# Two more weight slots, in room that GpSimd's transfer scratch held: one layer of gated mixers and experts on one core

## The chip, the core and the metric

The kernel runs on one core of a Trainium2 chip. The metric is the device time of one execution in microseconds (us), taken as the median of several runs. A profile is one further execution, recorded instruction by instruction. The engines are PE (matrix products), DVE (vector), ACT (scalar), POOL (GpSimd) and SP (which here only issues transfers).

## The reference, cut to what matters

Sequence 256, width 1024, one layer: two token mixers side by side, then 32 experts in 4 groups, of which each token takes the best group and in it the best two experts.

```
h = rmsnorm(x, norm1_g)
u, v_a, q, k, v_b = split(h @ w_in)              # w_in 1024 x 5120
y_a = chunked_spatial_gating(u, v_a, ...)        # u * (tril(w_s) rmsnorm(v) + b), chunks of 128
y_b = rmsnorm(diff_attention(rms(q), rms(k), v_b)) * (1 - lam_init)
g_a, g_b = split(sigmoid(h @ w_gate + b_gate))
merged = g_a * (y_a @ w_up_a) + g_b * (y_b @ w_up_b)
x = x + merged @ w_out
h2 = rmsnorm(x, norm2_g)
x = x + hierarchical_moe(h2, w_rg, b_rg, w_re, b_re, w1, w3, w2)
# expert e: ((silu(h2 @ w1[e]) * (h2 @ w3[e])) * c[e]) @ w2[e], 1024 -> 256 -> 1024, all in float32
```

## The kernel before, in words

All weights are read once: 136 chunks of 1 MB (128 partitions x 2048 float32, 8 KB per partition), 40 of the dense products (`wf`) and 96 of the experts (`wm`: 8 groups of 4 experts, 12 chunks each, of which 8 hold w1 and w3 and 4 hold w2). I number the experts' chunks c0 to c95, so that group g has c(12g) to c(12g+11).

Room on chip is a list of slots of 8 KB per partition, handed out in the order in which they came free. `NSLOT = 20` slots are there from the start; 3 of them serve the split halves of weights (`hl`), the other 17 serve chunks, x and its parts, and `hl` as well when the three are taken. Later parts of the program add slots where other buffers end. `Stream.pump(reserve)` issues the next chunk's load on SP's queue as long as more than `reserve` slots are free; RESERVE gives that number phase by phase, 6 at the start and 0 or 1 later. So how far the loads run ahead of the products is the number of slots, and the order in which they stand in SP's queue is fixed when the program is written out (a manual schedule). SP's transfers use eight semaphores in turn, so that a load is issued only when the load eight places ahead of it has landed. Room that the gates leave is handed on as four pieces of 2 KB, and a chunk that goes there is loaded by four transfers of 256 KB (line 121); all other chunks go by line 123, and the very last one by two halves (line 115).

The program has two stages. In the dense stage (to about 269 us) every product is made in three passes: a half chunk (a unit) is split into `hl`, the high part by ACT (line 339), the low part by DVE (line 343), of units 12 to 43 the last 352 columns by POOL (line 345). PE uses both in lines 355 to 359 and 384 to 386. Attention heads, norms and constants are hung between the units. `wst`, the spatial mixer's weights, is loaded at unit AT by line 239, and POOL masks it in line 244 and makes further constants in lines 245 to 249, ahead of its next part of a split.

In the expert stage PE gathers a group's tokens (line 976), makes h from 8 chunks (line 1025, 8 products a chunk), turns `hid` (`pt`, line 1039), makes y from 4 chunks (line 1067, 16 products a chunk) and adds it to the result (line 1046). A chunk's slot is handed back right after its products, and the next load is issued there. In the last group 20 small products on constants follow each chunk of h (`wps`, line 215) and 10 more the last, which keep PE at work. `pv` holds the gains per partition, 128 x 43; ACT's first split of x (line 306) reads it.

```
    def pump(self, reserve):
        while self.i < len(self.srcs) and len(self.slots.free) > reserve:
```

Of the kernel before, what the change touches and what calls it, by code (L numbers as in the profile page):

```python
# [5 lines left out]
F32 = mybir.dt.float32  # L6
F32R = mybir.dt.float32r
BF16 = mybir.dt.bfloat16
# [7 lines left out]
P = 128  # L16
D = 1024
# [6 lines left out]
NWARM = 35          # products before the first operands are there  # L24
GLO, GPART = (12, 44), 352      # units of whose low parts GpSimd makes so many columns
# places of the steps of an attention head, in units of the dense products
# [9 lines left out]
NSLOT = 20          # slots of 8 KB per partition  # L36
RESERVE = (6, 3, 2, 0, 0, 0, 0, 0, 1)     # slots kept free of weights, phase by phase
SL = 32             # token slots of an expert in a round
NW = (20, 10)
# columns of the result in the weight chunks of w2: the last chunk comes and is used in two parts, on different banks  # L40
COLS = (((0, 256),), ((512, 256),), ((256, 128), (768, 128)), ((384, 128), (896, 128)))
NGRP = 8            # groups of four experts on the tensor engine
NCH = 12            # weight chunks of a group
ROUNDS = T // SL

# columns of the per-partition vectors
# [3 lines left out]
class Slots:  # L50
    """Slots of 8 KB per partition, handed out in the order in which they were freed; some are four pieces of 2 KB."""
# [21 lines left out]
    def take_chunk(self):  # L73
        """Room for a weight chunk, as tile or as four."""
        if isinstance(self.free[0][1], str):
            return self.take([P, 2048], F32, "w")
        s = self.free.pop(0)
        self.k += 1
        t = tuple(s[0].tile([P, 512], F32, tag=tag, name=f"w_{self.k}_{i}") for i, tag in enumerate(s[1]))
        self.owner[id(t)] = (s, t)  # L80
        return t
# [5 lines left out]
    def give(self, other):  # L87
        """All free slots to another."""
        other.free += self.free
        self.free = []  # L90


def piece(chunk, e):
    """An expert's part of a weight chunk."""
    return chunk[e] if isinstance(chunk, tuple) else chunk[:, e * 512:(e + 1) * 512]


class Stream:
    """Loads of weight chunks, issued in order as slots become free."""
# [6 lines left out]
    def pump(self, reserve):  # L106
        while self.i < len(self.srcs) and len(self.slots.free) > reserve:
            src = self.srcs[self.i]
            if self.i == len(self.srcs) - 1:        # in columns, to be used one after the other
                if all(not isinstance(tag, str) for _, tag in self.slots.free):  # L110
                    break
                t = self.slots.take([P, 2048], F32, "w")
                c = 0
                for _, w in COLS[-1]:
                    self.nc.sync.dma_start(t[:, c * 8:(c + w) * 8], src[:, c * 8:(c + w) * 8])
                    c += w
            else:
                t = self.slots.take_chunk()
                if isinstance(t, tuple):
                    for e in range(4):  # L120
                        self.nc.sync.dma_start(t[e], src[:, e * 512:(e + 1) * 512])
                else:
                    self.nc.sync.dma_start(t, src)
            self.ready.append(t)
            self.i += 1

    def claim(self):
        """A slot for the next chunk, whose load the caller issues."""
        t = self.slots.take([P, 2048], F32, "w")
        self.ready.append(t)  # L130
        self.i += 1
        return t
# [16 lines left out]
def body(tc, cp, sp, tp, mmp, axp, xT_d, xn_d, wf_d, wm_d, wst_d, bs_d, pv_d, rb_d, wr_d, out_d):  # L149
# [11 lines left out]
    # Pools of a part of the program, on memory that others use before and after.  # L161
# [22 lines left out]
    stream = Stream(nc, slots, [wf_d[i] for i in range(40)] + [wm_d[g, c] for g in range(NGRP) for c in range(NCH)])  # L184
    pv = cp.tile([P, PV_N], F32, name="pv")
    nc.gpsimd.dma_start(pv, pv_d)
# [18 lines left out]
    # the tensor engine's clock rises while it works: let it, before the first operands are there  # L205
# [16 lines left out]
    # key - query for the keys of the first query tile, then of the second; far below zero where masked  # L222
# [6 lines left out]
    utri = cp.tile([P, P], BF16, name="utri")   # 1 where row < column  # L229
# [12 lines left out]
    def late_consts():  # L242
        # causal mask of the spatial weights: s <= t
# [12 lines left out]
    em = cp.tile([P, NT], F32, name="em")       # EPS / r1^2, r1 the first norm's factor  # L256
    rbc = fp.tile([P, T], F32, name="rbc")      # r1 along the free axis, on all partitions
    nlam = cp.tile([P, 1], F32, name="nlam")    # -(lambda)
# [51 lines left out]
    # A unit takes half a weight chunk, split two units ahead. Other work is queued for a unit's place.  # L310
# [50 lines left out]
    def add_nat(ab, name, done, res, pre=None):  # L361
        """512 columns of a product, tokens on partitions: a result for each token tile."""
# [10 lines left out]
    def add_T(ab, name, done, res, pre=None):  # L373
        """256 columns of a product, columns on partitions: [P, 2, T]."""
# [16 lines left out]
    def norm_a(pss, name):  # L391
        """Squares of pss."""
        sqs = []
        for t in range(len(pss)):
            sq = t2k([P, 512], f"sq_{name}{t}")
            S.activation(sq, pss[t], AF.Square)
            sqs.append(sq)
        return sqs

    def norm_r(sqs, n, d, scaled, name):  # L400
        """1 / root mean square of the n groups of d in the rows, of their squares; scaled: of rows still to be multiplied by r1,
        with that factor (r1 rsqrt(r1^2 ss / d + EPS) = rsqrt(ss / d + EPS / r1^2))."""
# [51 lines left out]
    KL = 3 * P      # keys of the first query tile, then those of the second  # L454
    TS = (slice(0, P), slice(P, KL))

    def attn_head(h, off):
        st = {}

        def s0():  # L460
            sc = st["sc"] = qp.tile([P, 2, KL], F32, tag="t3k", name=f"sc{h}", bufs=2)
            pss = [ax_ps(f"sc{h}{c}") for c in range(2)]
            for t in range(NT):     # the two halves side by side, on 64 rows each
# [193 lines left out]
    def swap():  # L657
# [6 lines left out]
        def park(half):  # L664
            """x into PSUM, until the residual is added."""
# [9 lines left out]
        # gates, pair of columns by pair; the merged product takes their place  # L675
# [35 lines left out]
    def to_router():  # L711
        """The memory of the temporaries: a slot, and the router's weights."""
# [20 lines left out]
    def x1_T(t, half, pts):  # L733
        """The transpose of half a token tile of x1, by way of parts of PSUM."""
# [14 lines left out]
    def o_done(pss):  # L749
        def a():  # L750
            A["acc"] = slots.take([P, NT, D], F32, "acc")   # x, then x + out, then that / rms
# [23 lines left out]
    res = [[None] * 2 for _ in range(NT)]       # the result, summed up in PSUM  # L775

    def res_init(t, half):
        """x1 into the result; x1 / rms, without the gain, takes its place."""
# [12 lines left out]
    def choose(t):  # L791
        """Steps of the choice of group and experts."""
# [43 lines left out]
    for q in range(4):      # the second half: only split here  # L836
        units.append(Unit(q % 2, None, None, None, 1 if q == 1 else RESERVE[8]))

# [44 lines left out]
    def gates_free(j):  # L883
        """Half of the merged product's memory, for weights."""
# [3 lines left out]
    # the first token tile is finished earlier than the second  # L888
# [4 lines left out]
    tail[0]()       # x + out, first half  # L893
# [5 lines left out]
    tail[1]()       # and its transposes  # L899
# [23 lines left out]
    def choice_end(sel, gather0, evac0):  # L923
        """The end of the choice of experts, of the second token tile mostly, and the first group's first half."""
# [26 lines left out]
    def put_out(c, n):  # L951
        """n columns of the result."""
# [10 lines left out]
    def group(g, chunks, done, mid, store):  # L963
        """Gathers the tokens of group g, in parts; then its products."""
# [30 lines left out]
        def gather0(t, part):  # L995
            """The first half in two parts, token tile by tile: the bank is cleared by the first product only."""
# [23 lines left out]
        def products():  # L1020
# [32 lines left out]
            for i, ranges in enumerate(COLS):  # L1053
# [3 lines left out]
                for part in [(r,) for r in ranges] if final else [ranges]:  # L1057
# [19 lines left out]
                    if store and i < 2:     # no other work to wait for  # L1077
# [33 lines left out]
    def consume(st):  # L1111
        """The next chunk of a stream; and what gives its slot back and loads ahead."""
# [13 lines left out]
    def rest():  # L1126
        for t in range(NT):
            weights(t)
        # number of further rounds
# [29 lines left out]
def prep(i):  # L1159
# [7 lines left out]
    def nat(w, nb):   # 512 columns -> 2 chunks [128, 4 kc, 512]  # L1167
        return w[:, nb * 512:(nb + 1) * 512].reshape(2, 4, P, 512).transpose(0, 2, 1, 3).reshape(2, P, 2048)

    def tr(w):        # -> chunks [128, 2 cc, 8 kc, 128]  # L1170
# [8 lines left out]
    wm = np.empty((NGRP, NCH, P, 4, 2, 256), np.float32)        # w1 and w3, then w2  # L1179
# [3 lines left out]
    w2 = A("w2")[..., cols].reshape(NGRP, 4, 2, P, 4, 256).transpose(0, 4, 3, 1, 2, 5)   # g, chunk, p, e, f, 256  # L1183
# [3 lines left out]
    for _, n in COLS[-1]:     # the last chunk's parts one after the other  # L1187
# [32 lines left out]
```

## Time and profile before

| | us |
|---|---|
| median of 3 runs | 475.11 |
| the runs | 476.5, 475.11, 473.06 |
| profiled execution, span | 469.4 |
| PE busy in it | 439.8 (94%) |
| DVE, ACT, POOL busy | 208.4, 175.4, 92.0 |
| chain that ended last | PE 66%, DMA 29% |
| read from HBM | 147.14 MB, mean 316 GB/s |

The profiled execution has no time of its own beside its span: the span runs from the first instruction to the last, and 5.7 us lie between it and the median of the runs (475.11 - 469.4). A share of busy time is a mean over both stages, which have different limits; the rows further down are therefore taken stretch by stretch. In them "out<-in" names tiles, "x8" counts instructions of one kind in a row, and what stands in brackets is the engine's idle time ahead of the first of them and what ended it.

### The profile page before, as it was taken

To read this page: it belongs to the slowest core of one execution; us is meant where nothing else is said; L and a number is where in the kernel's file an instruction comes from. 1 tells how busy PE (TensorE), PEld (TensorE's weight loads), DVE (VectorE), ACT (ScalarE), POOL (GpSimd) and SP (SyncE) were. 2 spreads that over 40 slices of the span, in tenths; PEclk is the share of its full clock that TensorE was granted. 3 is DMA by queue.
4 is the path that set the end of the run, shared out by engine and by line. 5 is a ranking of instruction groups with operands and counts; after the bars stand their busy time and mean duration, and the time that the engine had idled before them with its cause. 6 is when DMAs were issued, how large, how long until landed. Compare 5 with 4: busy or idle time off the path is not lost.

```text
span 469.4 us, 8478 instructions
## 1 busy us (share of the span) xinstructions
PE 439.8 (94%) x3446; PEld 335.5 (71%) x3446; DVE 208.4 (44%) x389; ACT 175.4 (37%) x332; POOL 92.0 (20%) x119
## 2 busy tenths in 40 slices
PE   8999999999999999999999988989889898959984
PEld 7878778878999999999988734554636464426553
DVE  4575687779897555555775641011111111110012
ACT  6646657776554664433455322010101010001001
POOL 2047665455757000003000100000000000000000
PEclk9999999999999999999999999999999999998998
DMA  7999960540237967788676989999999999999993
GB/s 252 371 422 417 420 278 5 181 177 2 90 96 276 417 220 271 311 318 345 243 305 265 339 342 426 419 422 406 416 420 418 422 406 420 420 421 420 405 381 94
DMA packets 28206, 148.81 MB, mean 317 GB/s; under 512 B 3184, under 2 KB 6016, under 8 KB 12160
## 3 DMA queue, kind: packets, MB, share of 16 engines
q1 hardware_dynamic: 28128, 148.18, 79.6%
q8 instruction: 29, 0.48, 0.4%
q14 instruction: 17, 0.14, 0.1%
q0 software_dynamic: 32, 0.02, 0.1%
HBM read 147.14 MB, written 1.05 MB: 316 GB/s over the span
## 4 chain that ended last, share of the span: by engine, by line
PE 66%; DMA 29%; DVE 2%; ACT 1%; SPq 1%; issue 1%; ACTq 0%; DVEq 0%
DMA w<-in_wm_dram 24%; DMA w<-in_wf_dram 5%; PE h L1025 4%; PE y L1067 3%; PE res L1046 3%; PE gp L976 2%; PE wps L215 2%; PE v L355 2%; PE u L384 2%; PE a L385 2%; PE a L384 2%; PE gb L384 2%; PE ga L386 2%; PE b L386 2%; PE b L385 2%; PE b L384 2%
## 5 line engine op out<-in xcount | busy, mean ns | idle before, releaser
L343 DVE TENSOR_TENSOR hl<-w,hl 128x1024 fp32r<-128x1024 f32 (+2 forms) x88 | 91.2, 1040 | 62.7 <-ACT hl L339 62.2
L339 ACT CAST hl<-w 128x1024 fp32r<-128x1024 f32 (+1 forms) x88 | 84.6, 969 | 83.8 <-PE a L386 12.8
L1025 PE MATMUL h<-w,hT 128*32 128x512 f32 x512 | 62.4, 599 | 4.2 <-DMA w<-in_wm_dram 4.2
L984 DVE TENSOR_TENSOR hT<-gp,pv 128x512 f32<-128x512 f32 (+1 forms) x19 | 11.3, 606 | 103.0 <-PE gp L976 103.0
L345 POOL TENSOR_TENSOR hl<-w,hl 128x352 fp32r<-128x352 f32 x32 | 40.7, 1278 | 23.7 <-ACT hl L339 21.2
L1067 PE MATMUL y<-w,hidT 128*32 128x256 f32 (+1 forms) x528 | 34.6, 391 | 5.0 <-issue 3.7
L1073 ACT COPY yy<-y 128x256 f32<-128x256 f32 (+1 forms) x33 | 12.1, 366 | 70.1 <-PE y L1067 70.0
L976 PEld LDWEIGHTS gp<-Sg,acc 128*128 128x128 f32 x256 | 30.4, 192 | 9.2 <-issue 8.0
L1011 POOL TENSOR_TENSOR Sw<-Sg,C 128x128 f32<-128x128 f32 x16 | 6.1, 399 | 157.0 <-PE res L1046 142.7
L1046 PE MATMUL res<-yy,SwT 128*128 128x128 f32 (+1 forms) x192 | 34.8, 324 | 1.1 <-ACT yy L1073 1.0
L1046 PEld LDWEIGHTS res<-yy,SwT 128*128 128x128 f32 x192 | 25.9, 191 | 12.3 <-issue 6.7
L976 PE MATMUL gp<-Sg,acc 128*128 128x128 f32 x256 | 32.1, 279 | 2.1 <-DVE Sg L972 2.1
L1025 PEld LDWEIGHTS h<-w,hT 128*32 128x32 f32 x512 | 13.0, 109 | 29.2 <-issue 15.7
L1067 PEld LDWEIGHTS y<-w,hidT 128*32 128x32 f32 x528 | 16.0, 112 | 17.4 <-issue 8.7
L1035 ACT ACTIVATE hid<-h 128x256 f32<-128x256 f32 x8 | 3.1, 383 | 59.0 <-PE h L1025 59.0
L1036 DVE TENSOR_TENSOR hid<-hid,h 128x256 f32<-128x256 f32 x8 | 3.4, 422 | 35.7 <-ACT hid L1035 35.7
L384 PE MATMUL u<-xh,hl 128*128 128x256 f32 x64 | 18.8, 293 | 0.0
L215 PEld LDWEIGHTS <-ones_b 128*128 128x128 bf16 x205 | 13.2, 106 | 7.8 <-issue 6.7
L384 PE MATMUL ga<-xh,hl 128*128 128x256 f32 x64 | 18.2, 285 | 0.0
L386 PE MATMUL ga<-xh,hl 128*128 128x256 f32 x64 | 18.1, 283 | 0.0
L386 PE MATMUL b<-ybh,hl 128*128 128x256 f32 x64 | 18.1, 283 | 0.0
L386 PE MATMUL a<-yah,hl 128*128 128x256 f32 x64 | 18.1, 283 | 0.0
(220 smaller groups left out, 957.3 us busy)
## 6 DMA issues: line engine op xcount, KB each, us to landing
w<-in_wm_dram SPq DMA_DIRECT2D x87, 1024.0 KB, 12.6
w<-in_wf_dram SPq DMA_DIRECT2D x36, 1024.0 KB, 9.5
w<-in_wm_dram SPq DMA_DIRECT2D x32, 256.0 KB, 9.0
w<-in_wf_dram SPq DMA_DIRECT2D x8, 256.0 KB, 4.5
w<-in_wf_dram SPq DMA_DIRECT2D x4, 512.0 KB, 8.7
xT<-in_xT_dram SPq DMA_DIRECT2D x8, 128.0 KB, 4.5
xn<-in_xn_dram SPq DMA_DIRECT2D x1, 1024.0 KB, 9.2
xs<-in_xn_dram SPq DMA_DIRECT2D x1, 1024.0 KB, 8.9
```

The costliest lines, as they stand in the source:

```text
L215: TE.matmul(wps[:, :P], ones_b, ones_b, start=True, stop=True)
L339: S.copy(hl[:, 0, c], raw[:, c])
L343: V.tensor_tensor(hl[:, 1, c.start:m], raw[:, c.start:m], hl[:, 0, c.start:m].bitcast(F32), ALU.subtract)
L345: G.tensor_tensor(hl[:, 1, m:c.stop], raw[:, m:c.stop], hl[:, 0, m:c.stop].bitcast(F32), ALU.subtract)
L384: TE.matmul(o, wh, ah[:, kc], start=kc == 0, stop=False)
L385: TE.matmul(o, wh, al[:, kc], start=False, stop=False)
L386: TE.matmul(o, wl, ah[:, kc], start=False, stop=kc == KC - 1)
L976: TE.matmul(ps[:, i * P:(i + 1) * P], h2[:, t, kc * P:(kc + 1) * P], st["S"][:, t].rearrange("p e s -> p (e s)"), start=start, stop=t == N ...
L1025: TE.matmul(ps[e * SL:(e + 1) * SL], st["h"][kc // 4][:, kc % 4, e * SL:(e + 1) * SL], piece(w, e), start=kc == 0, stop=kc == KC - 1)
L1046: TE.matmul(res[t][c // 512][:, c % 512:c % 512 + n], st["SwT"][:, t * P:(t + 1) * P], yy[:, o:o + n], start=False, stop=True, skip_group_ ...
L1067: TE.matmul(py[e * SL:(e + 1) * SL, :n], hidT[:, f, e * SL:(e + 1) * SL], w[e][:, f], start=f == 0, stop=f == 1)
L1073: S.copy(yy, py[:, :n])
```

## The change

Three edits. The memory that the program sets aside for descriptors of transfers issued by GpSimd goes from 16 KB per partition (the default) to 1 KB. The load of `pv`, the only transfer that GpSimd issued, is issued on ACT's queue instead. And NSLOT goes from 20 to 22, so that two more slots of 8 KB lie in what was scratch. The rest of the diff takes comments out and changes no line number.

```diff
-NSLOT = 20          # slots of 8 KB per partition
+NSLOT = 22
...
     pv = cp.tile([P, PV_N], F32, name="pv")
-    nc.gpsimd.dma_start(pv, pv_d)
+    nc.scalar.dma_start(pv, pv_d)
     xT = slots.take([P, KC, T], F32, "xT")
...
-    nc = _bacc.Bacc("TRN2", target_bir_lowering=False, num_devices=1)
+    nc = _bacc.Bacc("TRN2", target_bir_lowering=False, num_devices=1, dynamic_dma_scratch_size=1024)
```

On ACT, at the start of the program, the load of `pv` now comes first; the table load and the copy `warm_a` are there only to have the activation table in place:

```order
 L1216 UNCONDITIONAL_BRANCH
+L186 DMA pv<-in_pv_dram 128x43
 L210 ACT_TABLE_LOAD
 L210 COPY warm_a<-warm_a 128x1
```

It moved from POOL, whose first instruction after the constants of the frame it was. No other instruction changed its engine.

On SP, before, ten chunks by line 123 (they follow the four chunks that the start loads by halves and quarters) stand ahead of `wst`:

```order
L123 DMA w_260<-in_wf_dram 128x2048
L123 DMA w_281<-in_wf_dram 128x2048
L123 DMA w_304<-in_wf_dram 128x2048
L123 DMA w_306<-in_wf_dram 128x2048
L123 DMA w_308<-in_wf_dram 128x2048
L123 DMA w_341<-in_wf_dram 128x2048
L123 DMA w_378<-in_wf_dram 128x2048
L123 DMA w_454<-in_wf_dram 128x2048
L239 DMA wsb_109<-in_wst_dram 128x1024
```

Now, from the same load (the third by line 123) on:

```order
L123 DMA w_260<-in_wf_dram 128x2048
L123 DMA w_262<-in_wf_dram 128x2048
L123 DMA w_264<-in_wf_dram 128x2048
L123 DMA w_285<-in_wf_dram 128x2048
L123 DMA w_308<-in_wf_dram 128x2048
L123 DMA w_310<-in_wf_dram 128x2048
L123 DMA w_312<-in_wf_dram 128x2048
L123 DMA w_345<-in_wf_dram 128x2048
L123 DMA w_382<-in_wf_dram 128x2048
L123 DMA w_458<-in_wf_dram 128x2048
L239 DMA wsb_109<-in_wst_dram 128x1024
```

Two chunks more stand ahead of `wst`, twelve in place of ten; the numbers in names only count tiles.

On SP, before, the loads ahead of the router's bias and weights (`rb`, `wr`, near the end of the dense stage) are the last three dense chunks and six of the experts':

```order
L123 DMA w_1933<-in_wf_dram 128x2048
L123 DMA w_1964<-in_wf_dram 128x2048
L123 DMA w_2025<-in_wf_dram 128x2048
L123 DMA w_2086<-in_wm_dram 128x2048
L123 DMA w_2118<-in_wm_dram 128x2048
L123 DMA w_2120<-in_wm_dram 128x2048
L123 DMA w_2151<-in_wm_dram 128x2048
L123 DMA w_2211<-in_wm_dram 128x2048
L123 DMA w_2217<-in_wm_dram 128x2048
L719 DMA rb<-in_rb_dram 128x40
L720 DMA wr<-in_wr_dram 128x320
```

Now, at the same place:

```order
L123 DMA w_1937<-in_wf_dram 128x2048
L123 DMA w_1968<-in_wm_dram 128x2048
L123 DMA w_2029<-in_wm_dram 128x2048
L123 DMA w_2090<-in_wm_dram 128x2048
L123 DMA w_2122<-in_wm_dram 128x2048
L123 DMA w_2124<-in_wm_dram 128x2048
L123 DMA w_2155<-in_wm_dram 128x2048
L123 DMA w_2215<-in_wm_dram 128x2048
L123 DMA w_2221<-in_wm_dram 128x2048
L719 DMA rb<-in_rb_dram 128x40
L720 DMA wr<-in_wr_dram 128x320
```

The same number of loads stands there, but each is of a chunk two places further on in the sequence. This holds for the rest of the program: before, 23 of the experts' chunks are loaded ahead of the first load that follows an expert product (line 1025), now 25.

## Rows read from the trace of the kernel before

**Rows 1.** The page's part 2: 40 slices of equal length, first to last.

```profile
PEclk9999999999999999999999999999999999998998
...
GB/s 252 371 422 417 420 278 5 181 177 2 90 96 276 417 220 271 311 318 345 243 305 265 339 342 426 419 422 406 416 420 418 422 406 420 420 421 420 405 381 94
```

**Rows 2.** Busy time of engines, granted clock, DMA share, GB/s, by stretch.

```profile
270.00:281.00 11.00, 8.94 (x70) 3.58 (x63) 4.67 (x25) 3.15 (x8) 0.80 (x2) 1.00 0.88 339
...
308.00:419.00 111.00, 99.31 (x936) 55.34 (x940) 13.42 (x30) 10.84 (x29) 3.78 (x10) 1.00 1.02 417
419.00:434.00 15.00, 13.23 (x118) 7.83 (x122) 1.54 (x3) 1.87 (x5) 0.75 (x2) 0.89 1.01 421
```

**Rows 3.** PE's timeline, 372 to 435 us: start, duration, instruction, idle before.

```profile
372.91 0.44 PE L1039 MATMUL pt<-ident,hid 128*128 128x128 f32 x2 [1.02 <-DVE hid L1036]
...
394.45 0.44 PE L1039 MATMUL pt<-ident,hid 128*128 128x128 f32 x2 [1.02 <-DVE hid L1036]
395.52 1.93 PE L1067 MATMUL y<-w,hidT 128*32 128x256 f32 x32 [0.63 <-issue]
...
408.97 1.07 PE L1025 MATMUL h<-w,hT 128*32 128x512 f32 x8 [0.40 <-DMA w<-in_wm_dram]
411.45 1.06 PE L1025 MATMUL h<-w,hT 128*32 128x512 f32 x8 [1.42 <-DMA w<-in_wm_dram]
413.94 1.07 PE L1025 MATMUL h<-w,hT 128*32 128x512 f32 x8 [1.43 <-DMA w<-in_wm_dram]
...
418.91 1.07 PE L1025 MATMUL h<-w,hT 128*32 128x512 f32 x8 [0.93 <-DMA w<-in_wm_dram]
421.00 0.44 PE L1039 MATMUL pt<-ident,hid 128*128 128x128 f32 x2 [1.02 <-DVE hid L1036]
422.07 3.80 PE L1067 MATMUL y<-w,hidT 128*32 128x256 f32 x32 [0.63 <-DVE hidT L1041]
...
433.68 1.07 PE L1025 MATMUL h<-w,hT 128*32 128x512 f32 x8
```

**Rows 4.** The chain that ended last, in order of time: start, duration.

```profile
397.72 21.15 DMA w<-in_wm_dram
```

**Rows 5.** SP's DMA queue, 352.5 to 372.6 us.

```profile
352.60 7.77 SPq L123 DMA_DIRECT2D w<-in_wm_dram  x4
...
372.46 0.33 SPq L123 DMA_DIRECT2D w<-in_wm_dram  x1
```

**Rows 6.** PE's timeline, 443 to 452 us.

```profile
449.44 1.07 PE L1025 MATMUL h<-w,hT 128*32 128x512 f32 x8
```

**Rows 7.** Issues of line 121, 440.1 to 440.5 us, and their landing.

```profile
L121 SPq DMA_DIRECT2D w<-in_wm_dram x1: 328/328/328, 440.2 to 440.2; - x1
...
DMA to landing us min/median/max: 9.0/9.0/9.0
```

**Rows 8.** SP's DMA queue, 12 to 60 us.

```profile
32.27 0.33 SPq L239 DMA_DIRECT2D wsb<-in_wst_dram  x1
```

**Rows 9.** POOL's timeline, 50 to 56 us.

```profile
51.00 1.10 POOL L244 TENSOR_SCALAR_AFFINE_SELECT wsb<-wsb 128x1024 f32<-128x1024 f32 x1 [1.25 <-DMA wsb<-in_wst_dram]
...
53.26 0.95 POOL L345 TENSOR_TENSOR hl<-w,hl 128x352 fp32r<-128x352 f32 x1
54.37 1.61 POOL L345 TENSOR_TENSOR hl<-w,hl 128x352 fp32r<-128x352 f32 x1 [0.16 <-DMA w<-in_wf_dram]
```

**Rows 10.** DVE's timeline, 53 to 56 us.

```profile
54.33 0.86 DVE L343 TENSOR_TENSOR hl<-w,hl 128x672 fp32r<-128x672 f32 x1 [1.51 <-ACT hl L339]
```

**Rows 11.** PE's timeline, 30 to 60 us.

```profile
30.36 1.25 PE L425 MATMUL pt_q<-ident,qn_q 128*128 128x128 f32 x8 [0.80 <-DVE qn_q L417]
...
59.06 0.62 PE L359 MATMUL k<-hl,xh 128*128 128x512 f32 x2
```

**Rows 12.** ACT's timeline, 0 to 30 us.

```profile
5.39 0.51 ACT L306 ACTIVATE xh<-xT,pv 128x256 fp32r<-128x256 f32 x1 [1.08 <-DMA pv<-in_pv_dram]
...
27.39 2.00 ACT L339 CAST hl<-w 128x1024 fp32r<-128x1024 f32 x2 [2.08 <-DMA w<-in_wf_dram]
```

## The prediction

> **What bounds the kernel now.** I read the page's slices first, for the limits of the two stages. The transfers run at 405 to 426 GB/s early and again from about 281 us on, and between them at 2 to 345 with a few slices above [rows 1]: in the dense stage the queue is full, then stops for want of slots, and PE has all it needs. In the expert stage the stretches give 339 GB/s and a DMA share of 0.88 at 270 to 281 us, then 417 GB/s and 1.02 to 419 us [rows 2]: a transfer is always under way. Which of the two, PE or the stream, is late at a given place, PE's timeline tells. One group to the next takes 394.45 - 372.91 = 21.54 us, with no wait on a transfer; then PE waits four times on a chunk, 0.40 + 1.42 + 1.43 + 0.93 = 4.18 us, and reaches `pt` of the next group at 421.00 [rows 3]. By its own pace it would have been there at 394.45 + 21.54 = 415.99, so the waits cost 5.01. The stream needs 2.48 us per chunk: eight loads are in flight, each issued when the load eight ahead landed, and the issues at 352.60 and 372.46 are eight chunks apart, 19.86 / 8 [rows 5]. Twelve chunks take it 29.8 us, where PE takes 21.54. PE thus lives on a lead that the dense stage gave the stream, eats 8.3 us of it per group, and has used it up in group 6. From there to c91, the last chunk of h, the stream decides.
>
> PE's clock is the second thing. It was granted 0.89 of full speed at 419 to 434 us [rows 2]: the first 32 products of y there took 3.80 us, where the same 32 a group earlier took 1.93 [rows 3]. That is the lower of the two levels (1.2 GHz in place of 2.4), right after the four waits; price 1.87 us.
>
> **The change, part by part.** *Two slots more.* In the dense stage each load takes the slot that the load two places ahead of it took before, so the sequence runs two chunks ahead at every place, and the time of these two transfers is found where the queue stood still for want of slots. A chunk of the expert stage therefore lands 2 x 2.483 = 4.97 us sooner (by 417 GB/s a chunk takes 1.0486 MB / 417 = 2.51 us, two 5.03). I walk this along PE:
> - c79, the last wait: landed 397.72 + 21.15 = 418.87 [rows 4], now 413.90. PE by its own pace wants it at 415.99 - (421.00 - 418.91) = 413.90. All four waits go, just so.
> - y of group 6 starts at 422.07 - 5.01 = 417.06. c80 lands 2.48 behind c79, at 416.38, in time. c81 lands at 418.87 and is wanted after half of 1.93, at 418.02, so some 1.0 us of a new wait with its signal. The four waits ahead of it are gone, so I keep the clock at full speed.
> - group 7 starts at 433.68 - 5.01 - 1.87 + 1.0 = 427.80. Its chunks of h pace PE at (449.44 - 433.68) / 7 = 2.25 us with their small products [rows 3, 6], so PE wants c91 at 443.6.
> - c91 was issued at 440.2 and landed 9.0 later, 449.2 [rows 7], now 444.2. It decides: PE's last chunk of h starts at about 444.24 in place of 449.44 [rows 6]. From there on the end is PE's own chain and moves with it.
>
> Gain 5.20 us: the four waits and the slow clock, less what c91 still holds back.
>
> The Trainium skill, "DMA: Bandwidth & Descriptors", section "Where 436 GB/s comes from", holds a transfer from HBM to SBUF to about 358 GB/s per core. By that, as an estimate, two chunks are worth 5.86 us. The stretch at 417 GB/s disagrees, and the sum goes by the trace [rows 2].
>
> *`wst` behind two more chunks.* The loads ahead of `rb` and `wr` are other chunks, but are issued into the slots that came free there before: nothing. But `wst` stands behind twelve chunks in place of ten, in the one stretch of the dense stage where the queue is full (420 and 417 GB/s) [rows 1]. It was issued at 32.27 [rows 8], and POOL waited 1.25 us for it, to 51.00 [rows 9]. Now it lands 4.97 later, and POOL's mask starts at 55.97. Behind it on POOL stand the constants and then the low part of unit 16, which started 53.26 - 51.00 = 2.26 after the mask: now at 58.23. It took 0.95, and the next one, beside a DVE split that ran from 54.33, took 1.61 [rows 9, 10]. So it ends at 59.2 to 59.85, and PE wants it at 59.06 [rows 11]. Loss 0.1 to 0.8 us; I take 0.5, since DVE splits the next unit at about that time. PE bounds this stage, and the loss goes on to the end, because the first slots that the expert products free come as much later.
>
> The Trainium skill, "SBUF — State Buffer", section "Who interferes with whom", says that a DVE instruction with two SBUF inputs contends with a GpSimd instruction that reads SBUF. By it the low part would take the 1.61 and the loss be 0.8; the 0.95 with DVE idle and the 1.61 beside it agree [rows 9, 10], but nothing here fixes which of the two it will meet.
>
> *`pv` on ACT's queue.* ACT's first split waited 1.08 us for it, to 5.39 [rows 12]. From ACT it can be issued at 0.80 in place of 1.30. Its price lies between +1 us (it takes one of the eight semaphores, so that SP's eighth load waits for its landing) and -1.1 (the wait goes). Both ends are hidden: PE stands 0.80 us at 30.36 for q's norm [rows 11], which comes behind ACT's cast at 27.39, which waited 2.08 us for a chunk [rows 12]. The stream sets that place, and the stream has the same bytes to bring. I take 0, with 0.2 either way. The smaller scratch costs nothing that the trace shows, as no transfer is left to use it.
>
> Sum against the profiled span: 469.4 - 5.2 + 0.5 = 464.7. With the 5.7 us that lie between that span and the median of the runs: **470.4**.
>
> **The rivals.**
> - *The clock falls all the same.* The new wait for c81 or the hand-over of `hid` (1.02 us idle ahead of `pt`) [rows 3] brings the lower level in group 6's y. Group 7 then starts 1.87 later, PE wants c91 at 445.4, after its landing, and the gain shrinks to about 4.2: 471.4. For it: the clock fell at exactly this place. Against: it fell after those four waits, and a group earlier, with `pt` alone, it stood.
> - *The start pays.* `pv` lands a microsecond sooner, the stream of the start moves with it, and `wst` costs nothing, its chunks having filled an early gap: 469.4 - 5.2 - 0.9 = 463.3, so 469.0.
> - *It doesn't do what it says.* The two chunks wait in the sequence anyway (a semaphore or a reserve, not a slot, holds the loads back when the lead is made), and the lead at 270 us is as before: 474 to 476. Against: the queue stood nearly still for whole slices in the dense stage (2 and 5 GB/s) [rows 1], which only slots explain.
> - *Slower: `wst` is late by more than two chunks.* The twelfth load may have to wait for a slot that a split in the dense stage frees, with `wst` behind it on SP; POOL then holds unit 16, and PE pays one for one what `wst` is late beyond the 4.85 us that unit 16 had (59.06 - 53.26 - 0.95) [rows 9, 11]. When it lands later than some 61.0 us, it has cost over 5.2, and the kernel is slower: each further microsecond is one. Against: the slot of before's tenth load was free when its turn came, so the twelfth's should be too.
>
> **How the numbers follow.** Chances: forecast 0.57 (469.9 to 470.9), the clock 0.15, the start 0.15, no effect 0.07, slower 0.04, something else 0.02. The range is 468.3 to 473.0: the forecast, the clock and the start, with the bounds of `wst` and `pv` and some noise of the runs, which spread by 3.4 us. One per cent is 4.75 us, about what a measurement of this kernel can tell from no change; the bound lies at 470.36, in the middle of the forecast. So faster has half the forecast's chance, the start's and a little of the clock's: 0.47; same the other half, the clock's and that of no effect: 0.49; slower by over 1% 0.04.
>
> **What would show it.** Right: the chunks c79 and c91 land about 5 us sooner; no wait of PE at c75 to c79, and one of about 1 at c81; the 32 products of y in group 6 take 1.93; PE's last chunk of h starts at about 444.7; POOL's mask at 56 and a gap of half a microsecond in PE at 59. Wrong: the lead at 270 us is not two chunks longer; PE is slow somewhere with the memory as it is now; or the loads of the start, with `pv` among them, leave PE's first product later than 5.95 by more than the 0.8 that it stands at 30.36.

## The result and the profile after

The changed kernel takes 468.64 us (median of 6 runs, 466.6 to 470.27) against 474.36 for the kernel before (6 runs, 471.78 to 476.5): a ratio of 0.9892, interval 0.9864 to 0.992. A second measurement of the same kernel, below, gives 0.9918 (0.9886 to 0.9949). The profiled execution has a span of 466.7 us, 2.7 under the 469.4 of before. That is about half of what the medians differ by (5.7), and the reason for it is part of what follows.

The page's part 2 of the changed kernel answers [rows 1]:

```profile
PEclk9999999999999999999999998999999999999998
...
GB/s 244 344 425 421 416 402 105 180 179 2 93 91 268 322 312 271 213 364 302 310 239 303 315 326 407 422 418 421 406 418 420 421 418 413 412 421 419 422 382 88
```

The two chunks show as the 402 and 105 GB/s in the sixth and seventh slice, where before stood 278 and 5: the queue runs on for longer before it stops for want of slots. From the 26th slice on the rates are those of before. The lower clock of the 37th slice is gone, and there is a lower one in the 25th, which before did not have.

PE's timeline of the changed kernel, 285 to 450 us, answers [rows 3, 6]:

```profile
289.85 3.25 PE L1067 MATMUL y<-w,hidT 128*32 128x256 f32 x32 [0.52 <-DVE hidT L1041]
...
397.80 0.44 PE L1039 MATMUL pt<-ident,hid 128*128 128x128 f32 x2 [1.02 <-DVE hid L1036]
...
410.85 3.64 PE L1025 MATMUL h<-w,hT 128*32 128x512 f32 x32
...
416.40 1.92 PE L1025 MATMUL h<-w,hT 128*32 128x512 f32 x16
419.34 0.44 PE L1039 MATMUL pt<-ident,hid 128*128 128x128 f32 x2 [1.02 <-DVE hid L1036]
420.41 1.94 PE L1067 MATMUL y<-w,hidT 128*32 128x256 f32 x32 [0.63 <-issue]
...
444.16 1.06 PE L1025 MATMUL h<-w,hT 128*32 128x512 f32 x8 [0.19 <-DMA w<-in_wm_dram]
...
446.64 1.07 PE L1025 MATMUL h<-w,hT 128*32 128x512 f32 x8 [0.19 <-DMA w<-in_wm_dram]
```

From 397.80 to 419.34 it takes 21.54 us, PE's own pace, where before took 26.55 (421.00 - 394.45). All four waits are gone: the 32 products from 410.85 on run in one piece, as do the 16 from 416.40 on. The products of y after them take 1.94 in place of 3.80. And PE waits 0.19 for each of the last two chunks of h, c90 and c91: the stream is just late there. c91 starts at 446.64 in place of 449.44, 2.80 sooner, which is about the difference of the spans.

Where the other 2.4 of the 5.2 us stayed is seen early. SP's queue, POOL's timeline (57 to 60.6 us) and PE's timeline of the changed kernel answer [rows 8, 9, 11]:

```profile
15.04 19.76 SPq L123 DMA_DIRECT2D w<-in_wf_dram  x12
36.89 0.33 SPq L239 DMA_DIRECT2D wsb<-in_wst_dram  x1
```

```profile
57.18 1.10 POOL L244 TENSOR_SCALAR_AFFINE_SELECT wsb<-wsb 128x1024 f32<-128x1024 f32 x1 [7.02 <-DMA wsb<-in_wst_dram]
...
59.77 0.92 POOL L345 TENSOR_TENSOR hl<-w,hl 128x352 fp32r<-128x352 f32 x1
```

```profile
30.01 0.66 PE L425 MATMUL pt_q<-ident,qn_q 128*128 128x128 f32 x4 [1.12 <-DVE qn_q L417]
31.64 0.65 PE L425 MATMUL pt_q<-ident,qn_q 128*128 128x128 f32 x4 [0.98 <-DVE qn_q L417]
...
60.75 0.73 PE L359 MATMUL k<-hl,xh 128*128 128x512 f32 x2 [0.83 <-DVE nm L471]
```

`wst` is issued behind twelve chunks, POOL waits for it until 57.18, and PE stands 0.83 us at 60.75. The row names DVE as what ended this wait, but POOL's low part of unit 16 ended at 60.69, just ahead of it, and in the run with `wst` one chunk later, below, the row of the same products names POOL; I read it as POOL's. Before that PE has waited twice at q's transposes, where before waited once. In the same place in its sequence PE is 0.7 us later than in the profile of before after q's transposes, 1.8 behind the wait at 60, 2.1 at 90 and 2.1 at the first expert product; the first load that follows it is issued at 272.93 in place of 270.83, 2.1 later as well.

### The profile page after: what moved, and what is told of

Its sections match the earlier page's. It is cut to its first block, busy times and chain, and to the rows that moved or that the text cites. A ratio compares the mean times of both kernels' runs of the same rounds, so it can differ in the third digit from the quotient of the medians.

```text
span 466.7 us, 8463 instructions
## 1 busy us (share of the span) xinstructions
PE 438.9 (94%) x3446; PEld 334.8 (72%) x3446; DVE 207.4 (44%) x389; ACT 175.3 (38%) x332; POOL 94.7 (20%) x118
## 4 chain that ended last, share of the span: by engine, by line
PE 81%; DMA 7%; DVE 3%; ACT 3%; issue 2%; POOL 1%; SPq 1%; ACTq 0%
PE h L1025 10%; PE y L1067 7%; PE gp L976 6%; PE res L1046 6%; DMA w<-in_wm_dram 4%; DMA xn<-in_xn_dram 2%; PE v L355 2%; PE u L384 2%; PE ga L386 2%; PE b L386 2%; PE b L385 2%; PE b L384 2%; PE a L386 2%; PE a L385 2%; PE a L384 2%
## 5 line engine op out<-in xcount | busy, mean ns | idle before, releaser
L385 PE MATMUL ga<-xl,hl 128*128 128x256 f32 x64 | 18.1, 283 | 0.0
L384 PE MATMUL gb<-xh,hl 128*128 128x256 f32 x64 | 18.1, 283 | 0.0
```

Of the source, the lines that this page charges most:

```text
L384: TE.matmul(o, wh, ah[:, kc], start=kc == 0, stop=False)
L385: TE.matmul(o, wh, al[:, kc], start=False, stop=False)
```

## The experiments

Each ratio is to the kernel before, timed on the same chip, with its 95% interval. A fifth of a per cent is 1 us.

**The change once more.** No edit.

> The changed kernel once more, for what of its profile repeats. If the losses of the dense stage belong to the change, PE is again 1.3 to 2.1 us later than in the kernel before at 90 us, with a wait at q's second transposes (31 us) and one at 60 us; the span is 465 to 467. If they were chance, one or both are gone and the span is 463.5 to 465. Ratio 0.987 to 0.992 in both cases.

Ratio 0.9918 (0.9886 to 0.9949). The span, 467.5, lies above both of the ranges that I gave. PE is late again, by 1.3 us at q's second transposes and by 2.7 at 35 us, since its granted clock is 0.50 at 32 to 35 us. But the wait at 60 us is missing. POOL's and PE's timelines of this run:

```profile
56.29 1.10 POOL L244 TENSOR_SCALAR_AFFINE_SELECT wsb<-wsb 128x1024 f32<-128x1024 f32 x1 [4.08 <-DMA wsb<-in_wst_dram]
...
58.55 2.97 POOL L345 TENSOR_TENSOR hl<-w,hl 128x352 fp32r<-128x352 f32 x3
```

```profile
61.82 0.39 PE L359 MATMUL k<-hl,xh 128*128 128x512 f32 x1
```

POOL is as late as in the first profile of the change, less 0.9, but PE itself comes to the last products on unit 16's low part later still, at 61.82, without a wait. So, as far as these two profiles tell, the loss at the start and the loss through `wst` do not add up: the larger one counts, since one hides the other.

**The kernel before once more.** No edit, one profile.

> The kernel before once more, for what of its profile repeats. If the profiled execution of before was a lucky one at the start, PE is 0.5 to 1.4 us later at 31 us here and the span is 470 to 472, about 2 us under the median of the runs, as in the other profiles. If it was not, the span is 469.4 within half a microsecond.

The span is 472.3 and the execution took 473.97. PE's timeline of this run:

```profile
289.75 3.47 PE L1067 MATMUL y<-w,hidT 128*32 128x256 f32 x32 [0.52 <-DVE hidT L1041]
...
415.52 1.06 PE L1025 MATMUL h<-w,hT 128*32 128x512 f32 x8 [1.42 <-DMA w<-in_wm_dram]
...
420.50 1.07 PE L1025 MATMUL h<-w,hT 128*32 128x512 f32 x8 [0.93 <-DMA w<-in_wm_dram]
...
423.89 3.64 PE L1067 MATMUL y<-w,hidT 128*32 128x256 f32 x32 [0.63 <-DVE hidT L1041]
```

The stretches (busy times, then granted clock, DMA share, GB/s):

```profile
285.00:295.00 10.00, 7.81 (x60) 3.78 (x57) 0.85 (x2) 2.78 (x5) 0.59 (x2) 0.78 0.97 401
```

The waits of group 6 and its slow products of y are there again. But the products of y in group 0 took 3.47 us, at a clock of 0.78; the profile that the prediction was made from has 1.94 there. At 31 us PE was 0.2 us later than in it. So the expectation held for the span (472.3, just over the 470 to 472 expected), not for the place: the execution that the prediction was made from was 2.9 us shorter than this one, and the first place where PE parts by more than a microsecond is group 0, through its clock: 0.5 us at the first expert product, 2.0 ahead of these products of y, since products of h were slow as well, and 3.6 behind them. Span and time are 1.7 us apart here, not the 5.7 of my sum. This 1.7 (1.66 to 1.84) lies between the time and the span of each run whose span is on record; in the other profiles of this study the span is 1.0 to 2.9 under the median of its runs, but for one with 0.2.

**`pv` on ACT's queue and the small scratch alone.**

```diff
-NSLOT = 22
+NSLOT = 20
```

> The change without the two slots: 20 slots, pv on ACT's queue, scratch of 1 KB. If the slots carry the gain, PE waits on c75 to c79 as before and the time is within 1% of the kernel before (ratio 0.995 to 1.006), with PE 0 to 1.3 us late at 31 us through the changed start. If the queue of pv or the smaller scratch carries it, most of the 5.7 us is here already: ratio about 0.99.

Ratio 1.0008 (0.9984 to 1.0032). PE's timeline of this run, 400 to 435 us:

```profile
410.81 1.07 PE L1025 MATMUL h<-w,hT 128*32 128x512 f32 x8 [1.42 <-DMA w<-in_wm_dram]
...
420.75 1.07 PE L1025 MATMUL h<-w,hT 128*32 128x512 f32 x8 [0.93 <-DMA w<-in_wm_dram]
```

The waits are those of before. So neither the queue of `pv` nor the scratch gains or costs anything that can be measured. PE started 0.7 us sooner (5.21) and was 0.8 us later at 31.

**The two slots alone.** `pv` is issued by GpSimd again, out of the scratch of 1 KB.

```diff
-    nc.scalar.dma_start(pv, pv_d)
+    nc.gpsimd.dma_start(pv, pv_d)
```

> The change without the move of pv: 22 slots, scratch of 1 KB, pv still issued by GpSimd. If the slots carry the gain, ratio 0.985 to 0.991 to the kernel before, no wait of PE on c75 to c79, and the wait behind POOL's mask at 59 us, about 1 us, stays. If the start as changed by pv also costs something on its own (PE was 1.4 us late at q's transposes in the profile of the change), PE is level with the kernel before at 31 us here and the time is about 1 us under that of the change. If pv carries it, ratio 1.0.

Ratio 0.9889 (0.9857 to 0.9921): the whole gain. PE's timeline, 400 to 450 us:

```profile
417.77 0.44 PE L1039 MATMUL pt<-ident,hid 128*128 128x128 f32 x2 [1.02 <-DVE hid L1036]
...
420.74 1.94 PE L1067 MATMUL y<-w,hidT 128*32 128x256 f32 x16 [0.82 <-DMA w<-in_wm_dram]
...
446.84 1.07 PE L1025 MATMUL h<-w,hT 128*32 128x512 f32 x8
```

No wait on c75 to c79, but 0.82 on c81, as the prediction had it (1.0). The 16 products behind that wait took 1.94 in place of 1.07: the clock fell all the same. c91 starts at 446.84, much as in the change (446.64), but not for the same reason: here PE does not wait for it. The issue of c91's load, 425.5 to 426 us, and its landing:

```profile
L123 SPq DMA_DIRECT2D w<-in_wm_dram x1: 328/328/328, 425.6 to 425.6; - x1
...
DMA to landing us min/median/max: 19.8/19.8/19.8
```

It had landed at 445.4, and PE came 1.4 us after it, late by the slow products. PE was 1.4 us late at 31 us here too, with `pv` issued as before, so the move of `pv` is not what makes it late.

**One slot.**

```diff
-NSLOT = 22
+NSLOT = 21
```

> The change with 21 slots in place of 22. If each slot is worth one chunk of the stream, 2.48 us at c91, the ratio to the kernel before is about 0.9945 (0.992 to 0.997), with waits of PE in group 6 that sum to about 2 us. If the lead matters as a whole (enough or not enough), it is 0.989 or 1.0.

Ratio 0.9945 (0.9917 to 0.9973), about the half. PE's timeline, 400 to 435 us:

```profile
413.09 1.06 PE L1025 MATMUL h<-w,hT 128*32 128x512 f32 x8 [0.21 <-DMA w<-in_wm_dram]
...
418.07 1.06 PE L1025 MATMUL h<-w,hT 128*32 128x512 f32 x8 [0.93 <-DMA w<-in_wm_dram]
...
421.22 3.80 PE L1067 MATMUL y<-w,hidT 128*32 128x256 f32 x32 [0.63 <-DVE hidT L1041]
```

Waits of 0.21 and 0.93 are left of four, and the slow products of y are there. The interval leaves out both 1.0 and the first measurement of the change (0.9892), but not the second (0.9918).

**Two slots fewer than before.**

```diff
-NSLOT = 20          # slots of 8 KB per partition
+NSLOT = 18          # slots of 8 KB per partition
```

> The kernel before with 18 slots. If each slot is worth one chunk, c91 lands 4.97 us later and the ratio is 1.009 to 1.012, with PE's waits starting a good half group earlier than c75. If the dense stage starves for want of slots too, PE has waits on dense chunks between 60 and 270 us and the ratio is over 1.015. If the slots are worth nothing in this direction, 1.0.

Ratio 1.0101 (1.006 to 1.0142). PE's timeline, 395 to 435 us:

```profile
398.48 1.07 PE L1067 MATMUL y<-w,hidT 128*32 128x256 f32 x16 [0.60 <-DMA w<-in_wm_dram]
...
409.38 1.07 PE L1025 MATMUL h<-w,hT 128*32 128x512 f32 x8 [0.95 <-DMA w<-in_wm_dram]
...
411.87 1.06 PE L1025 MATMUL h<-w,hT 128*32 128x512 f32 x8 [1.05 <-DMA w<-in_wm_dram]
...
424.37 1.07 PE L1025 MATMUL h<-w,hT 128*32 128x512 f32 x8 [0.24 <-DMA w<-in_wm_dram]
```

PE meets the stream earlier, at 398.48 (the second chunk of y in group 5), and up to 281 us it is level with the kernel before, so the dense stage does not starve. With 18, 20, 21 and 22 slots the ratios are 1.0101, 1, 0.9945 and 0.9892 or 0.9918: about half a per cent for each slot, 1.9 to 2.6 us, where a chunk of the stream is 2.48.

**The clock held in group 6.** Small products on constants behind the chunks of h of group 6, in the kernel before; first 20 behind each chunk from the third on.

```diff
-                if store:
+                if store or (g == NGRP - 2 and kc > 1):
                     warm(NW[0])
```

> The kernel before, with 20 small products on constants behind each chunk of h of group 6 from the third on, as the last group has them. They should keep PE at work in its waits, and the 32 products of y in group 6 should take 1.93 us in place of 3.80. If the stream sets the time at c91, what PE saves before it is waited for there: ratio 0.998 to 1.001. If the slow clock is a term of its own, the 1.87 us come off: ratio 0.996.

Ratio 1.0016 (0.9993 to 1.0039). PE's timeline, 405 to 435 us:

```profile
427.27 1.93 PE L1067 MATMUL y<-w,hidT 128*32 128x256 f32 x32 [0.59 <-DVE hidT L1041]
```

The products of y took 1.93, so the clock held. But the small products took more of PE's time than the waits had been, so this run does not tell the theories apart. The next has 16 of them only where PE waited.

```diff
+                elif g == NGRP - 2 and kc in (3, 4, 6):
+                    warm(16)
```

> The kernel before, with 16 small products only behind c75, c76 and c78, where PE waits 1.4, 1.4 and 0.9 us in its profile, so that they take no time of PE's own. If they keep the clock, group 6's 32 products of y take 1.93 us. Then, if the stream sets the time at c91, ratio 0.998 to 1.001, with waits of PE on c89 to c91; if the slow clock is a term of its own, 0.996.

Ratio 1.0001 (0.9976 to 1.0026). PE's timeline, 405 to 455 us:

```profile
415.06 1.07 PE L1025 MATMUL h<-w,hT 128*32 128x512 f32 x8 [0.42 <-DMA w<-in_wm_dram]
...
423.14 1.07 PE L1069 MATMUL y<-w,hidT 128*32 128x256 f32 x16 [0.59 <-DVE hidT L1043]
425.08 1.07 PE L1069 MATMUL y<-w,hidT 128*32 128x256 f32 x16 [0.87 <-DMA w<-in_wm_dram]
...
447.74 1.06 PE L1025 MATMUL h<-w,hT 128*32 128x512 f32 x8 [0.16 <-DMA w<-in_wm_dram]
```

At full speed PE comes to c81 too early and waits 0.87 for it, and 0.16 for c90. In the kernel before, the slow clock is no term of its own: what PE saves there, it waits for the stream.

**`wst` two chunks earlier,** behind ten again, in the change.

```diff
-    at(AT[0], load_mix)
+    at(5, load_mix)
```

> The change with the load of wst and bs moved two chunks ahead, back to ten chunks by line 123. If the late mask costs PE about 1.1 us at 59 us and nothing gives it back, that wait is gone and the time is about 1 us below the change (ratio to the kernel before 0.985 to 0.989). If what is behind wst comes late instead, or the loss is given back in the expert stage, the time is that of the change (ratio 0.989) or above.

Ratio 0.9892 (0.9856 to 0.9928), that of the change. POOL's timeline, 50 to 62 us:

```profile
52.26 1.10 POOL L244 TENSOR_SCALAR_AFFINE_SELECT wsb<-wsb 128x1024 f32<-128x1024 f32 x1 [1.53 <-DMA wsb<-in_wst_dram]
...
54.52 0.94 POOL L345 TENSOR_TENSOR hl<-w,hl 128x352 fp32r<-128x352 f32 x1
```

The mask is 4.9 us earlier than in the change and PE does not stand at 60. PE was 1.3 us late at 31 us in this profile, so there was less for `wst` to cost. c91 starts at 445.54 in it, 1.1 us ahead of the first profile of the change; the runs, whose interval is 3.4 us wide, show no difference.

**`wst` one chunk later,** behind thirteen.

```diff
-    at(AT[0], load_mix)
+    at(12, load_mix)
```

> The change with wst and bs one chunk later still (thirteen chunks by line 123 ahead, in place of twelve). If the slower rival's mechanism holds (POOL's mask holds up the low part of unit 16, one for one), PE waits some 3.5 us at 59 to 60 us in the profile, against 0.8 to 1.0 in that of the change, and the time is 2.5 us above it: ratio to the kernel before 0.993 to 0.997. If the lateness is hidden or given back, the ratio is 0.989 to 0.991.

Ratio 0.9926 (0.9902 to 0.9951). PE's timeline, 58 to 62 us, names POOL:

```profile
61.92 0.50 PE L359 MATMUL k<-hl,xh 128*128 128x512 f32 x1 [1.78 <-POOL hl L345]
```

The wait is 1.78 in place of 0.83, on POOL's low part of unit 16. That is the mechanism of the slower rival, at half of the size that I expected. The time lies above both measurements of the change, but its interval overlaps with theirs. Nor is it `wst`'s alone in this profile: the clock fell in group 6 here, too, and PE came to c91 1.1 us after it had landed (449.36 and 448.25).

**One power for both token tiles,** with `wst` two chunks earlier: one GpSimd instruction of 16 columns in the norms of q and k in place of two of 8.

```diff
+        if m == 2 and n == 8:
+            rsqrt_g(f.rearrange("p t n -> p (t n)"), ss.rearrange("p t n -> p (t n)"), 16)
+        else:
+            for t in range(m):
+                rsqrt_g(f[:, t, :n], ss[:, t, :n], n)
```

> The change with wst and bs two chunks earlier, and the power of both token tiles in one GpSimd instruction in the norms of q and k. If q's norm, which waits for GpSimd's second power, is what makes PE late at 31 us, PE is 1 us or more earlier there than in the run with wst earlier alone, all of the rest moves with it, and the ratio to the kernel before is 0.985 to 0.988. If the first chunks or xn hold PE there anyway, the ratio is that of the change, 0.989.

Ratio 0.9925 (0.9897 to 0.9953). POOL's and PE's timelines of the start:

```profile
27.35 2.93 POOL L252 TENSOR_TENSOR f_q<-ss_q,mhalf 128x16 f32<-128x16 f32 x1
```

```profile
31.06 1.25 PE L429 MATMUL pt_q<-ident,qn_q 128*128 128x128 f32 x8 [1.78 <-DVE qn_q L421]
```

The one power took 2.93 us and PE stood 1.78 at q's transposes. PE was 0.7 us later there than in the first profile of the kernel before, against 1.3 in the run with `wst` earlier alone: 0.6 sooner, not the 1 us expected, and the time is not better. This profile says little of it, since the clock fell in group 6 again and PE came to c91 at 448.41, 2.9 us after it had landed. Nothing shows that it is a way to a faster kernel. None of these versions beats the change beyond the uncertainty of its own measurement.

## Why the prediction was right, step by step

**What bounds it, and what a slot is worth: right.** The mechanism is the stream's lead. The change without the slots gives 1.0008, the slots without the rest 0.9889, and from 18 to 22 slots the time falls by 1.9 to 2.6 us a slot, counted from 20. The four waits go, the products of y run at full speed, and c91 is where PE and the stream meet: all three stand in the profile after, and the wait for c81, which was to be 1.0, was 0.82 in the run with the slots alone. In the profile of the change it does not show because PE was 3.35 us later by then (397.80 against 394.45), 1.3 of them lost to the lower clock in group 0. Of its other signs, c79 and c91 were to land about 5 us sooner. Against the profile that the prediction was made from they land 2.8 and 2.5 sooner (416.11 and 446.60); against the second profile of the kernel before (420.45 and 452.03) it is 4.3 and 5.4. One reading behind the 2.48 us is not exact: of the eight loads that are issued from 352.60 on, ahead of 372.46, four are quarters of a chunk (line 121). The eight whose landings let them go were whole chunks, so the figure stands; the last two chunks of h in the profile after start 2.48 apart as well.

**The clock as part of the sum: right for the kernel before, open for the change.** I listed the 1.87 us of slow products among what is gained, and then let c91 decide. For the kernel before that holds: in the run with fitted products the clock held and nothing came off. For the change I kept the clock at full speed, since the four waits go. Of the six profiles with 22 slots the clock held in group 6 in three (the change twice, `wst` earlier). In these it had been lower in group 0 (0.84 granted at 282 to 293 us), which cost PE 1.3 to 1.5 us there; PE then came late enough not to wait for c81, and started c91 within 0.05 us of its landing. In the other three (the slots alone, `wst` later, one power) the clock was 1.00 at 282 to 293 us, PE waited 0.82 to 0.86 for c81, the 16 products behind it took 1.93 or 1.94 in place of 1.07, and PE came to c91 1.1 to 2.9 us after it had landed. So the rival that the clock falls all the same came true there, and with its price of a microsecond or more; that the profile of the change was spared it is luck, as PE had been slowed in group 0, where the stream's lead hid it. The wait does not decide it alone, since in the run with fitted products the clock held behind one of 0.87.

The medians hide this, but the single runs suggest that the clock counts: of the 24 runs of the change (both measurements), the slots alone and `wst` earlier, the 7 with a mean granted clock of 0.994 or more have a median of 467.5 us, the 4 with 0.987 or less one of 471.0. In which place it was lower there is not on record.

**`wst`: right in its place and mechanism, the size is not fixed.** POOL's mask, which was to start at 55.97, started at 57.18 and 56.29. PE stood 0.83 at 60 us (0.1 to 0.8 forecast, 0.5 taken), and a chunk more of lateness gave 1.78. But in two of three profiles of a kernel with `wst` behind twelve chunks PE did not stand there at all, because it came late itself. What I missed is that a fixed slack of 4.85 us was read from an early PE. With `wst` moved back to ten chunks, the runs show no difference that they can tell from none.

**`pv`: nothing, as taken.** PE's first product came 0.7 us sooner, at 5.27 (5.01 to 5.27 in the seven profiles with `pv` on ACT's queue, 5.33 to 6.04 in the six with `pv` on GpSimd's), and the lead was lost by 31 us, as the prediction argued. The claim that nothing but the stream's chunk sets that place was too simple: it waits for the second power on GpSimd, too.

**The sum: two terms mis-sized, on opposite sides.** The step that failed is "with the 5.7 us that lie between that span and the median of the runs". The distance that I put on the span was 5.7 and it came out at 1.9: 1.7 lie between any run's time and its own span, and the other 4.0 are what that one execution was shorter than the median. On the other side, the span that I predicted was 464.7 and it came out at 466.7: PE was 2.1 us late at the first expert product, where the sum had 0.5 for `wst`. The two nearly cancel (470.4 forecast, 468.64 measured, and the gain of 5.7 us stands against 4.7), so that the sum comes as near as it does is in part luck. The cause is common to both: the profiled execution of before was a short one (469.4, against 472.3 in a second profile). Measured from the second profile, the change saves 5.6 and 4.8 us of span, about what the 4.97 of two chunks allow. Part of what makes one execution faster than another at the start is the order of two instructions, which the last section shows; why the clock falls in group 0 in some and not in others I have not traced to a cause.

## What to carry to other kernels

Where a stream of transfers never rests, a buffer more is worth about one transfer's time at the place where the consumer catches up with it (here 1.9 to 2.6 us, with 2.48 a transfer); compute that place first. Waits and a slow clock ahead of it cost nothing only as long as the consumer still comes there before the transfer: in the kernel before, that time would otherwise have been waited for; with 22 slots a slow clock in group 6 made PE come 1.1 to 2.9 us late, and one in group 0 did not. A load that stands behind the stream in the same queue becomes later by each buffer that is added, so look for the engine that waits for it. And a sum that starts from one profile should have that profile's distance to the runs checked against another one: the distance was 1.0 to 2.9 us in most profiles here, and 5.7 in the one that I used, of which only 1.7 lie between a run's time and its own span.

## What the runs showed of the hardware that was not expected

GpSimd's power of 128 x 8 elements takes quite different times, by whether DVE's split began before it. POOL's timeline of the changed kernel at 24 to 32 and 63 to 66 us, and DVE's at 24 to 33 us:

```profile
25.51 2.24 POOL L252 TENSOR_TENSOR f_q<-ss_q,mhalf 128x8 f32<-128x8 f32 x1
...
28.21 2.65 POOL L252 TENSOR_TENSOR f_q<-ss_q,mhalf 128x8 f32<-128x8 f32 x1
...
63.65 1.65 POOL L252 TENSOR_TENSOR f_q<-ss_q,mhalf 128x8 f32<-128x8 f32 x1
```

```profile
25.54 1.29 DVE L343 TENSOR_TENSOR hl<-w,hl 128x512 fp32r<-128x512 f32 x2
28.13 1.23 DVE L343 TENSOR_TENSOR hl<-w,hl 128x1024 fp32r<-128x1024 f32 x1 [1.30 <-ACT hl L339]
...
30.89 0.69 DVE L417 TENSOR_TENSOR qn_q<-q,f_q 128x512 f32<-128x512 f32 x1 [0.94 <-POOL f_q L252]
```

The same two instructions of the kernel before, POOL's and DVE's timeline at 24 to 33 us:

```profile
27.91 1.65 POOL L252 TENSOR_TENSOR f_q<-ss_q,mhalf 128x8 f32<-128x8 f32 x1
```

```profile
28.47 1.22 DVE L343 TENSOR_TENSOR hl<-w,hl 128x1024 fp32r<-128x1024 f32 x1 [1.97 <-ACT hl L339]
```

At 63.65, where no DVE instruction runs beside it, the power takes 1.65 us. It takes 1.65 in the kernel before as well, where it starts 0.56 us ahead of the split and runs beside it. In the changed kernel it starts 0.08 us after the split and takes 2.65. Of the twelve profiles with a power of this size, the second power of q starts 0.03 to 0.25 us after the split in four, takes 2.49 to 2.69 and ends 1.5 us after the split's end; in the other eight it starts ahead of the split or after its end and takes 1.65. At a lead of 0.03 us it can go either way: the first power above takes 2.24, the second of the repeat of before 1.65. The Trainium skill, "SBUF — State Buffer", section "Who interferes with whom", says that a DVE instruction with two SBUF inputs contends with a GpSimd instruction that reads SBUF. The splits have both inputs in SBUF, and the four agree with that. In these four, DVE's second norm of q waits 0.94 us for POOL, and PE stands a second time at q's transposes. The run with the clock held is one of them, and up to group 6 it is the kernel before; so this wait does not belong to the change.

PE's clock falls in group 0 in some executions and not in others of the same kernel: 3.47 us for the 32 products of y in one profile of the kernel before, 1.94 in the other, and 3.25 in the changed kernel. Ahead of them PE always waits 1.67 us for DVE.
